# A pool of its own for late latents, one store per latent tile, tables split in the last pair, and the second modulation a step later

## Chip, cores and metric

The kernel runs on one core of one Trainium2 chip. The metric is device microseconds (us) for one execution of the whole kernel: one layer of a bidirectional encoder over two sequences, in one launch.

## What is computed

Two sequences of 1024 tokens with 1024 features go through one layer each, with the same weights and a conditioning vector of their own. Cut to what matters here:

```python
def layer(x, c, ...):
    mod = silu(c) @ w_ada + b_ada                       # six vectors of 1024
    sh1, sc1, ga1, sh2, sc2, ga2 = split(mod, 6)
    h = rmsnorm(x, g_mix) * (1 + sc1) + sh1
    z = h @ w_in
    q_lat, kv_lat, k_pe, f_in = split(z, (256, 128, 64, 512))
    y_mla = mla_group(q_lat, kv_lat, k_pe, ...)         # latent attention, 4 heads
    y_four = fourier_group(f_in, w_four)                # real part of a 2-D FFT per group of 64 features
    x = x + ga1 * (concat(y_mla, y_four) @ w_out)
    h2 = rmsnorm(x, g_ffn) * (1 + sc2) + sh2
    return x + ga2 * ((silu(h2 @ w_gate) * (h2 @ w_up)) @ w_down)
# y = rmsnorm(layer(x, c), g_final) for both sequences
```

## The kernel before

Products are made in three passes. Each fp32 operand is split into a rounded high part and a rest (`split`, L62 to L64: a copy on ScalarE at L63, a subtraction at L64 on VectorE unless another engine is named), and `mm3` (L79 to L81) issues high x high, high x rest and rest x high on TensorE.

**Stage 1**, up to about 216 us, computes h and z. It walks over eight pairs k = 0 to 7 (sequence s = k // 4, index j = k % 4); a pair holds two tiles of 128 tokens that the Fourier transform mirrors on each other. `zboth` makes the latent part of z for both tiles of a pair (448 columns: query latents, key-value latents, rotary key), from sums and differences of the two tiles (`eo`, in the trace `eoh` and `eol`); L467 and L469 bring the result to SBUF, L489 to L495 apply rotation and norm. `latents` transposes the result on TensorE (L519) and splits it (in the trace `lh` and `ll`, in the last pair `lhl`). The two halves, and those of the key-value latents (`kv`), go to DRAM (`lat_d`, `ckv_d`) by one transfer each; they are collected in a list and issued by `flush` (L510). `fourier_in(k, i)` multiplies the even (i = 0) or odd (i = 1) part of a pair with the folded weights and cosines of the feature transform (24 matmuls), and adds the result from PSUM into `zc` (i = 0) or `zs` (i = 1) by two VectorE operations (L545, L546). A product for the row of token 0 and its like (`zoc`, 24 matmuls, L559 to L565) follows the pair where the second sequence begins.

The last pair is written out by hand (from L783): `zboth(7)`, the splits of `zx` and of the cosine half `zh` with the subtraction on GpSimd, the transform of pair 6, the cast of `tcor`, the split of the first table `tb`, the transposes of pair 7, and the transform of pair 7 with the split of `zn`. The raw tables are loaded (L740, L744) into a pool `praw` that is opened at L730, after pool `p1b` has been closed at L728. `p1b` held, among others, the last latents of pairs 2 to 6 (`lat4`, tag `hf`).

**Stage 2** makes the transform over the tokens. `dft(s)` (L931) forms A (cosine part; q = 0, 2, 1 for sequence 0, where 2 is a narrow tile of 48 rows) and B (sine part) with tables `tb[0]` and `tb[1]`. For each q it fills two PSUM banks, `pe` and then `po`, taken in turn from a pool of eight. `zsplit` (L921) splits `zs` (in the trace `zsin`), the subtraction on GpSimd for sequence 0. `fourier_out(s, ..., j, g)` (L1007) multiplies A and B with folded output weights `wm`, in eight steps t per sequence; L1019 to L1022 bring the results to SBUF as `ea` and `ed`, and they go to DRAM (`fo_d`). Between these steps runs the second modulation: `mod2(c)` (L1046) for c = 0 to 7 takes a 1 MB chunk of `w_ada` (tile `wada2`, `wada` in the trace) and issues four matmuls of 32 x 512 (L1054). `mod2(c)` is called behind step t = c + 1 of sequence 0, `mod2(7)` in the middle of `dft(1)`; then L1110 copies the sum to `modrow`, and `mod_vecs` transposes it (L145) and makes the vectors of the second modulation. The chunks 0 to 2 are loaded ahead of `dft(0)` (L1059), behind `wq_l` (L1033).

Attention, output projection and FFN follow; the change doesn't touch them beyond the addresses of the latents in DRAM.

**Order of the work.** Each engine works through its instructions in one order. It follows the order of the code as far as data and buffers allow, and `issue_after` and `behind` hold a part back behind a named instruction. So a tile pool, which decides whose buffer is reused, and the place of a call both move instructions. SyncE (SP) issues nearly all transfers, in order as well: one that waits for its source holds up all behind it.

Of the kernel before, what the change touches and what calls it, by code (L numbers as in the profile page):

```python
# [21 lines left out]
P = 128  # L22
# [31 lines left out]
def hybrid_encoder_kernel(ctx: ExitStack, tc: tile.TileContext, a: dict):  # L54
# [68 lines left out]
    lat_d = [[dram.tile([P, 4, N], F32, name=f"lat_d{s}{i}") for i in range(2)] for s in range(2)]  # L123
    ckv_d = [[dram.tile([P, 8, KVL], F32, name=f"ckv_d{s}{i}") for i in range(2)] for s in range(2)]
# [35 lines left out]

    with ExitStack() as st:
# [34 lines left out]
        mods = {}  # L196
# [25 lines left out]
        def fold_loads():  # L222
            wukT = w.tile([P, HEADS, KVL], F32, tag="lh", name="wukT", bufs=2)
# [225 lines left out]
        def zboth(k, between):  # L449
# [12 lines left out]
            else:  # L462
                if k == 2:
                    st1["lat"] = w2.tile([P, 4, 512], F32, tag="hf", name="lat4", bufs=1)
# [3 lines left out]
            for u in range(2):  # L468
                nc.vector.scalar_tensor_tensor(out=sk[u][:, :DZ], in0=pz[1][:, :DZ], scalar=(0.5, -0.5)[u], in1=sk[1][:, :DZ],  # L469
                                               op0=ALU.mult, op1=ALU.add)  # L470
# [13 lines left out]
        def z_out(k, u, pz, sk, rz):  # L484
# [17 lines left out]
            for i in range(2):  # L502
                st1.setdefault("st", []).append((ckv_d[s][i][:, ti, :], rd(kv[:, i, :])))
# [8 lines left out]
        def latents(k, u):  # L512
# [7 lines left out]
            if k + 1 < nk:  # L520
                lh = w.tile([P, 512], F32R, tag="lh", name="lh", bufs=2)
                ll = w.tile([P, 512], F32R, tag="ll", name="ll", bufs=2)
            else:
                if u == 0:
                    st1["lhl"] = w.tile([P, 4, 512], F32R, tag="hh0", name="lhl")
                lh, ll = (st1["lhl"][:, 2 * u + i, :] for i in range(2))
            split(lh, ll, pl)
            for i, t in enumerate((lh, ll)):
                st1.setdefault("st", []).append((lat_d[s][i][:, :, ti * P : ti * P + P], rd(t).rearrange("p (a b) -> p a b", a=4)))
# [3 lines left out]
        def fourier_in(k, i):  # L533
# [10 lines left out]
            else:  # L544
                nc.vector.tensor_tensor(out=z[:, j, :], in0=z[:, j - 1, :], in1=pc[:, : n1 - n0], op=(ALU.subtract, ALU.add)[i])  # L545
                here["z"] = nc.vector.tensor_tensor(out=z[:, j - 1, :], in0=z[:, j - 1, :], in1=pc[:, : n1 - n0],  # L546
                                                    op=(ALU.add, ALU.subtract)[i]).ins
            if j == 1:
# [10 lines left out]
            if i == 1 and j == 0 and s == 1:  # L559
                po = bank()  # L560
                for c in range(NC):
                    mm3(po[:ZOW, :NZC], zoc[0][:, c, :], zoc[1][:, c, :], wcs_h[:, c, :NZC], wcs_l[:, c, :NZC],
                        c == 0, c == NC - 1)
                nc.vector.tensor_copy(zo, po[:ZOW, :NZC])
                nc.vector.tensor_copy(zc[0][0:1, 1, :], po[0:1, :NZC])  # L565

        def wide(tag, shape=(P, 4, 512)):
            return (w2 if tag == "hf" else w).tile(list(shape), F32, tag=tag, name="wide")
# [9 lines left out]
        wpe = w.tile([P, 2, HEADS * ROPE], F32, tag="lh", name="wpe", bufs=2)  # L578
# [20 lines left out]
        fold_out(1, wo2[0], wuvT, [w.tile([P, 512], F32, tag="ll", name="so", bufs=2) for g in range(2)])  # L599
# [19 lines left out]
        wf.clear()  # L619
        wt = [mod_load(6, cols0, wide("hh0")), mod_load(7, cols0, wada_tile())]  # L620
# [60 lines left out]
        def pair(k):  # L681
# [30 lines left out]
            if k + 1 < nk:  # L712
                next(st1["steps"], None)
# [15 lines left out]
        P2 = ExitStack()  # L729
# [5 lines left out]

        raws = {}
        for k, n in enumerate((NT, 512)):
            for c in range(2):
                raws[k, c] = raw_tile("raw")
                nc.sync.dma_start(raws[k, c][:, :n], a["tcos" if k == 0 else "tsin"][:, c, :])  # L740
        tb[0] = [wr.tile([P, 2, NT], F32R, name=f"tb0{i}") for i in range(2)]
        tcor = wr.tile([P, NTE], F32R, name="tcor")
# [1220 lines left out]
```

## Time and profile before

| | |
|---|---|
| median of 3 runs | 2057.08 us (2056.97 to 2059.08) |
| the profiled execution | 2061.09 us |
| its span in the trace | 2059.3 us |
| granted TensorE clock, mean | 0.995 |
| busy: PE / DVE / ACT / POOL | 2006.8 / 1397.6 / 890.2 / 831.9 us |
| first matmul of `dft(0)` | 215.67 us |
| first matmul of `fourier_out` | 230.69 us |
| first matmuls of the second modulation | 238.41 us |

Engines are named PE (TensorE matmul), DVE (VectorE), ACT (ScalarE), POOL (GpSimd), SP (SyncE). A row of the timeline gives the start in us, the time of the instructions, engine, line, operation, output<-input, shape, and, in square brackets, the idle time ahead and what ended it; x2 means that two like instructions stand in one row. A row of waits gives who waited for whom, the sum in us, the count and the longest. A row of windows gives the stretch, its length, then for PE, PEld (weight load), DVE, ACT and POOL the busy us and the count, the granted PE clock, the share of DMA and GB/s.

### The profile page before, as it was taken

Reading aid. Unit: us, or ns where it says so; the run is one execution under the profiler, and the core shown is the slowest. Engines: PE = TensorE matmul, PEld = TensorE weight load, DVE = VectorE, ACT = ScalarE, POOL = GpSimd, SP = SyncE. Lnnn points to the kernel's source line nnn. Section 1 sums busy time; section 2 is a strip of 40 time slices with the busy share of each in tenths; the row PEclk is TensorE's granted clock in tenths of the full one; section 3 lists DMA queues with packets and bytes.
Section 4 is the critical chain, followed back from the end, with each engine's and each line's share of the span. In section 5 each row is a group of like instructions: output and inputs, shape, how many; then the busy total and the mean of one; then the engine's idle time right before and its main releaser. Section 6 shows DMA issues by size and latency. Waiting matters only on the chain.

```text
span 2059.3 us, 28434 instructions
## 1 busy us (share of the span) xinstructions
PE 2006.8 (97%) x9910; PEld 1641.9 (80%) x9910; DVE 1397.6 (68%) x2071; ACT 890.2 (43%) x1732; POOL 831.9 (40%) x977
## 2 busy tenths in 40 slices
PE   6899899999999999999999999999999999999998
PEld 3778678888888877888888888877788888888876
DVE  4567658666676778667677676678665665667675
ACT  2664435555565564232333365453332333336441
POOL 0564313111313237878779410334544444420142
PEclk9999999999999999999999999999999999999999
DMA  9685884444544375555545587674322322258662
GB/s 387 252 317 178 288 319 112 133 93 104 147 113 143 134 261 200 183 173 179 200 158 185 172 299 254 214 234 166 133 89 90 116 90 103 99 182 277 219 221 96
DMA packets 183548, 376.64 MB, mean 183 GB/s; under 512 B 18508, under 2 KB 58060, under 8 KB 179564
## 3 DMA queue, kind: packets, MB, share of 16 engines
q1 hardware_dynamic: 166060, 321.34, 45.9%
q0 software_dynamic: 17344, 53.49, 8.6%
q8 instruction: 78, 1.28, 0.2%
q14 instruction: 66, 0.54, 0.1%
HBM read 262.75 MB, written 120.39 MB: 186 GB/s over the span
## 4 chain that ended last, share of the span: by engine, by line
PE 55%; DVE 3%; DMA 2%; POOL 1%; issue 1%; SPq 0%; ACT 0%; DVEq 0%; ACTq 0%; POOLq 0%
PE bank L81 19%; PE bank L80 19%; PE bank L79 18%; DVE wl L64 1%; DMA draw<-s_d 1%; DMA draw<-t_d 1%; DVE val L137 1%; DMA val<-x_d 0%; POOL val L137 0%; DVE val L1760 0%; DMA X<-hc_d 0%; ACT wh L63 0%; DVE val L134 0%; POOL rs_y L105 0%; SPq L1719 0%
## 5 line engine op out<-in xcount | busy, mean ns | idle before, releaser
L81 PE MATMUL bank<-H,wl 128*128 128x512 f32 x1232 | 490.4, 398 | 0.2 <-DVE wl L64 0.2
L80 PE MATMUL bank<-H,wh 128*128 128x512 f32 x1232 | 486.2, 395 | 0.3 <-DVE H L64 0.3
L79 PE MATMUL bank<-H,wh 128*128 128x512 f32 x1232 | 483.9, 393 | 2.2 <-DVE val L137 0.9
L79 PEld LDWEIGHTS bank<-H,wh 128*128 128x128 f32 x1232 | 231.3, 188 | 59.9 <-DVE val L137 1.8
L80 PEld LDWEIGHTS bank<-H,wh 128*128 128x128 f32 x1232 | 231.3, 188 | 59.7 <-DVE H L64 0.6
L81 PEld LDWEIGHTS bank<-H,wl 128*128 128x128 f32 x1232 | 231.2, 188 | 53.9 <-DVE wl L64 0.5
L64 DVE TENSOR_TENSOR wl<-draw,wh 128x512 fp32r<-128x512 f32 x286 | 202.1, 742 | 87.5 <-ACT wh L63 87.0
L137 DVE TENSOR_TENSOR val<-bank,val 128x512 f32<-128x512 f32 x200 | 136.6, 689 | 156.8 <-PE bank L81 153.1
L63 ACT CAST wh<-draw 128x512 fp32r<-128x512 f32 x286 | 168.4, 619 | 161.3 <-PE bank L80 90.5
L137 POOL TENSOR_TENSOR val<-val 128x512 f32<-128x512 f32 x58 | 83.3, 1444 | 367.2 <-DVE val L1734 192.9
L80 PE MATMUL bank<-wl,wh 128*128 128x512 f32 x572 | 223.8, 391 | 3.8 <-DVE wl L64 3.8
L79 PE MATMUL bank<-wh 128*128 128x512 f32 x572 | 222.7, 389 | 0.5 <-ACT wh L63 0.5
L63 ACT CAST wh<-rgu 128x512 fp32r<-128x512 f32 x172 | 106.7, 621 | 269.5 <-PE bank L80 209.4
L81 PE MATMUL bank<-wh,wl 128*128 128x512 f32 x572 | 222.7, 389 | 0.0
L63 ACT CAST wh<-val 128x512 fp32r<-128x512 f32 x133 | 82.1, 620 | 269.7 <-PE bank L80 256.2
L64 DVE TENSOR_TENSOR wl<-val,wh 128x512 fp32r<-128x512 f32 x133 | 135.5, 1021 | 75.8 <-ACT wh L63 75.7
L64 DVE TENSOR_TENSOR wl<-rgu,wh 128x512 fp32r<-128x512 f32 x172 | 165.4, 962 | 3.8 <-ACT wh L63 3.8
L134 POOL TENSOR_TENSOR val<-rgu 128x512 f32<-128x512 f32 x80 | 117.8, 1473 | 101.2 <-DMA rgu<-in_wgu_dram 87.0
L80 PEld LDWEIGHTS bank<-wl,wh 128*128 128x128 f32 x572 | 107.3, 188 | 29.4 <-DVE wl L64 7.4
L79 PEld LDWEIGHTS bank<-wh 128*128 128x128 f32 x572 | 107.4, 188 | 23.4 <-ACT wh L63 0.9
L81 PEld LDWEIGHTS bank<-wh,wl 128*128 128x128 f32 x572 | 107.4, 188 | 22.1
L1203 DVE TENSOR_REDUCE mx<-ps_s 128x1 f32<-128x1024 f32 x64 | 78.1, 1221 | 63.4 <-PE ps_s L1198 63.2
(388 smaller groups left out, 4051.5 us busy)
## 6 DMA issues: line engine op xcount, KB each, us to landing
rgu<-in_wgu_dram SPq DMA_DIRECT2D x86, 512.0 KB
draw<-s_d SPq DMA_DIRECT2D x143, 256.0 KB
s_d<-val POOLq DMA_DIRECT2D x88, 256.0 KB, 3.9
draw<-t_d SPq DMA_DIRECT2D x88, 256.0 KB
s_d<-val SPq DMA_DIRECT2D x66, 256.0 KB
draw<-in_w_down_dram SPq DMA_DIRECT2D x55, 256.0 KB
wada<-in_w_ada_dram SPq DMA_DIRECT2D x11, 1024.0 KB
xt<-in_x_dram SPq DMA_DIRECT2D x16, 512.0 KB
```

What stands on the lines that cost most here:

```text
L63: here["a"] = nc.scalar.copy(hi, src).ins
L64: here["v"] = (eng or nc.vector).tensor_tensor(out=lo, in0=src, in1=rd(hi), op=ALU.subtract).ins
L79: nc.tensor.matmul(out, lh, rh, start=first, stop=False, skip_group_check=cont)
L80: nc.tensor.matmul(out, lh, rl, start=False, stop=False, skip_group_check=cont)
L81: here["t"] = nc.tensor.matmul(out, ll, rh, start=False, stop=last, skip_group_check=cont).ins
L134: return eng.tensor_tensor(out=out, in0=x, in1=y, op=ALU.subtract).ins
L137: eng.tensor_tensor(out=out, in0=x, in1=y, op=ALU.add)
L1203: nc.vector.tensor_reduce(out=mx, in_=ps, axis=AX.X, op=ALU.max)
```

## The change

It does these things:

- A pool `p1c` is opened ahead of `p1b` and outlives it to the end of stage 2. It holds what had tag `hf`: the flipped tiles, `lat4`, one wide weight tile, and in stage 2 `wm00`, the first half of the output weights. `p1b` thus ends before the last pair, and `praw` opens with eight raw tiles first.
- Both halves of a latent tile lie in one tile (`lhl`, tag `lq`) and go to DRAM by one transfer; likewise for `kv`. That takes 32 transfers from stage 1.
- Ahead of `zboth(7)` now stand: the loads of the tables, of `wm00` and of `wnr`; the splits of `zx`, `zh` and of the first table; the cast of `tcor`. The subtractions of `zx`, `zh` and `zsin` go from POOL to DVE.
- The transposes of pair 7 go between `fourier_in(7, 0)` and `fourier_in(7, 1)`. The `zoc` product goes from pair 4 to pair 5.
- In stage 2 two of the eight PSUM banks get a tag of their own, `d`, for q = 0 of `dft` and for the sum of the second modulation.
- `mod2(c)` is called behind step t = c + 2, `mod2(6)` and `mod2(7)` in the middle of `dft(1)`. `wq_l` is loaded behind the first three chunks of `w_ada`. The first step of sequence 1 is held behind the copy to `modrow`, and `mod_vecs` behind that step's last product.

```diff
+    w3 = P2.enter_context(tc.tile_pool(name="p1c", bufs=1, side="right", reuse_waits="tile"))
...
-                st1["hf", k] = w2.tile([P, NC, 2, P], F32, tag="hf", name="hf", bufs=1)
+                st1["hf", k] = w3.tile([P, NC, 2, P], F32, tag="hf", name="hf", bufs=1)
...
-            for i in range(2):
-                st1.setdefault("st", []).append((ckv_d[s][i][:, ti, :], rd(kv[:, i, :])))
+            st1.setdefault("st", []).append((ckv_d[s][:, :, ti, :], rd(kv)))
...
-                lh = w.tile([P, 512], F32R, tag="lh", name="lh", bufs=2)
-                ll = w.tile([P, 512], F32R, tag="ll", name="ll", bufs=2)
+                both = w.tile([P, 2, 512], F32R, tag="lq", name="lhl", bufs=2)
...
-            for i, t in enumerate((lh, ll)):
-                st1.setdefault("st", []).append((lat_d[s][i][:, :, ti * P : ti * P + P], rd(t).rearrange("p (a b) -> p a b", a=4)))
+            st1.setdefault("st", []).append((lat_d[s][:, :, :, ti * P : ti * P + P],
+                                             rd(both).rearrange("p i (a b) -> p i a b", a=4)))
...
-            if i == 1 and j == 0 and s == 1:
+            if i == 0 and j == 1 and s == 1:
                 po = bank()
...
+        wmr0 = wm_loads(0, 0, 0)
+        table_load(1)
+        wnr0 = wn_load(0, 0, raw_tile("wnr")[:, :512])
+        split(zxs[0], zxs[1], zx)
+        z0 = zcos_split(0)
+        for c in range(2):
+            split(tb[0][0][:, c, :], tb[0][1][:, c, :], raws[0, c])
+        nc.scalar.copy(tcor, cor[:, :NTE])
         z = zboth(nk - 1, lambda c: flush() if c == 1 else None)
         next(z)
         flush()
-        with behind():
-            split(zxs[0], zxs[1], zx, nc.gpsimd)
-            z0 = zcos_split(0, nc.gpsimd)
-        wm0 = wm_half(0, 0, 0, wr)
-        wm1 = wm_loads(0, 0, 1), wn_load(0, 0, raw_tile("wnr")[:, :512])
+        wm1 = wm_loads(0, 0, 1), wnr0
         next(z, None)
         fourier_in(nk - 2, 0)
-        with behind():
-            nc.scalar.copy(tcor, cor[:, :NTE])
-            for c in range(2):
-                split(tb[0][0][:, c, :], tb[0][1][:, c, :], raws[0, c])
         fourier_in(nk - 2, 1)
+        fourier_in(nk - 1, 0)
         late_latents(nk - 1)
-        fourier_in(nk - 1, 0)
...
+        def bank2(tag="b"):
+            return pp.tile([P, 512], F32, tag=tag, name="bank", bufs=2 if tag == "d" else 6)
...
-                    split(zsin[0][:, c : c + 2], zsin[1][:, c : c + 2], zs[s][:, c : c + 2, :], nc.gpsimd if s == 0 else None)
+                    split(zsin[0][:, c : c + 2], zsin[1][:, c : c + 2], zs[s][:, c : c + 2, :])
...
-                pe, po = bank2(), bank2()
+                pe, po = (bank2("d" if q == 0 else "b") for _ in range(2))
...
-        nc.sync.dma_start(rd(wq_l), wq_d)
...
+        with behind():
+            wm0 = wm_half(0, 0, 0, None, wmr0)
...
         for c in range(3):
             mod2_load(c)
+        nc.sync.dma_start(rd(wq_l), wq_d)
         abn = dft(0)
...
-                    if t > 0:
-                        mod2(t - 1)
+                    if t > 1:
+                        mod2(t - 2)
...
                 def last_mod():
+                    mod2(NC - 2)
                     mod2(NC - 1)
-                    nc.vector.tensor_copy(mr, chunks.pop("ps"))
+                    here["mr"] = nc.vector.tensor_copy(mr, chunks.pop("ps")).ins
```

Two places show what moves. The first is DVE at the end of stage 1, around the last transform of pair 7 (`zc` and `zs` by two additions each) and the first splits of stage 2; rows before, from the split of the first table (`tb_2186`) to that of the second (`tb_2510`):

```order
L64 TENSOR_TENSOR tb_2186<-raw,tb_2185 128x514 x2
L64 TENSOR_TENSOR lhl<-bank,lhl 128x512
L64 TENSOR_TENSOR ll<-bank,lh 128x512
L545 TENSOR_TENSOR zc_111<-zc_111,bank 128x280
L64 TENSOR_TENSOR zn_2193<-zc_110,zn_2192 128x4x24
L546 TENSOR_TENSOR zc_111<-zc_111,bank 128x280
L545 TENSOR_TENSOR zs_113<-zs_113,bank 128x256
L64 TENSOR_TENSOR zn_2193<-zc_111,zn_2192 128x4x24
L546 TENSOR_TENSOR zs_113<-zs_113,bank 128x256
L64 TENSOR_TENSOR wm_2305<-wraw,wm_2304 128x512 x2
L64 TENSOR_TENSOR tb_2510<-raw,tb_2509 128x512 x2
```

The same additions now, up to the split of `wm00`:

```order
L547 TENSOR_TENSOR zc_107<-zc_107,bank 128x280
L548 TENSOR_TENSOR zc_107<-zc_107,bank 128x280
L64 TENSOR_TENSOR lhl<-bank,lhl 128x512 x2
L64 TENSOR_TENSOR zn_2151<-zc_106,zn_2150 128x4x24
L64 TENSOR_TENSOR zn_2151<-zc_107,zn_2150 128x4x24
L547 TENSOR_TENSOR zs_109<-zs_109,bank 128x256
L548 TENSOR_TENSOR zs_109<-zs_109,bank 128x256
L64 TENSOR_TENSOR zsin_2459<-zs_108,zsin_2458 128x512 x2
L64 TENSOR_TENSOR tb_2465<-raw,tb_2464 128x512 x2
L64 TENSOR_TENSOR wm_2470<-wraw,wm_2470 128x512 x2
```

The split of the first table has left this place: its two subtractions now stand some 14 rows ahead of `zc`, beside the rows in which the result of `zboth(7)` leaves PSUM. `zsin` is new on DVE, and `wm00` went behind the second table.

The second place is PE where the second modulation begins, among the products of `fourier_out` (`wm` with A, then with B); rows before, from the last three products of its second step to the first of the third:

```order
L79 MATMUL bank<-wm_2606,B_2529 128x512
L80 MATMUL bank<-wm_2607,B_2529 128x512
L81 MATMUL bank<-wm_2606,B_2530 128x512
L1054 MATMUL bank<-wada_2521,scT_2515 32x512 x4
L79 MATMUL bank<-wm_2304,A_2527 128x512
```

Now the first of them stands here, behind the first six products of the first step:

```order
L79 MATMUL bank<-wm_2470,A_2488 128x512
L80 MATMUL bank<-wm_2470,A_2488 128x512
L81 MATMUL bank<-wm_2470,A_2489 128x512
L1070 MATMUL bank<-wada_2481,scT_2475 32x512
L79 MATMUL bank<-wm_2567,B_2490 128x512
```

One of the four matmuls of `mod2(0)` has come 20 products forward, into the first step; the other three went back behind the third step. Before, all four stood together behind the second.

More of the change, by code (lines that the diff above doesn't have):

```diff
@@ L547, in fourier_in @@
                                                     op=(ALU.add, ALU.subtract)[i]).ins
+            if i == 0 and j == 1 and s == 1:
+                po = bank()
+                for c in range(NC):
+                    mm3(po[:ZOW, :NZC], zoc[0][:, c, :], zoc[1][:, c, :], wcs_h[:, c, :NZC], wcs_l[:, c, :NZC],
+                        c == 0, c == NC - 1)
+                nc.vector.tensor_copy(zo, po[:ZOW, :NZC])
+                nc.vector.tensor_copy(zc[0][0:1, 1, :], po[0:1, :NZC])
             if j == 1:
@@ L558, in fourier_in @@
                     nc.vector.tensor_copy(zoc[k][:, :, 2 * s : 2 * s + 2], rd(eo[1][k][:, :, 0:2]))
-            if i == 1 and j == 0 and s == 1:
[L560 to L565, printed above, removed]
         def wide(tag, shape=(P, 4, 512)):
-            return (w2 if tag == "hf" else w).tile(list(shape), F32, tag=tag, name="wide")
+            return (w3 if tag == "hf" else w).tile(list(shape), F32, tag=tag, name="wide")
         cols0 = [(0, 2048)]
@@ L751, in zcos_split @@
             return z
-        zn = [wr.tile([P, 4, NY2], F32R, name=f"zn{i}") for i in range(2)]
         def nyq_split():
@@ L895, in stage3_loads @@
         S["ld"] = last
-        S["ld2"] = [(rd(lat[i]), lat_d[0][i][:, 2:4, :]) for i in range(2)] + [(rd(ckv[i]), ckv_d[0][i]) for i in range(2)]
+        S["ld2"] = [(rd(lat[i]), lat_d[0][:, i, 2:4, :]) for i in range(2)] + [(rd(ckv[i]), ckv_d[0][:, i]) for i in range(2)]
         return rc, rs
@@ L1003, in prep_wm @@
                             st.enter_context(tc.issue_after(ins))
[L1004 to L1005 removed]
+                    halves = [wm_half(s, g, h, w, raw[h]) for h in range(2)]
+                    wms[s][g] = halves, list(wn)[-1]
         def fourier_out(s, ABn, j, g):
```

78 lines of the change are left out of this document (46 added, 32 removed).

## Prediction

> **What bounds the kernel now.** I read the page first: the busy times (part 1) and the chain that ended last (part 4).
>
> ```profile
> PE 2006.8 (97%) x9910; PEld 1641.9 (80%) x9910; DVE 1397.6 (68%) x2071; ACT 890.2 (43%) x1732; POOL 831.9 (40%) x977
> PE 55%; DVE 3%; DMA 2%; POOL 1%; issue 1%; SPq 0%; ACT 0%; DVEq 0%; ACTq 0%; POOLq 0%
> ```
>
> PE is busy for 2006.8 of 2059.3 us, so all its gaps together are 52.5 us, and PE leads the chain by far. The number and shapes of the matmuls stay as they are. So the time can only change by PE's gaps, by its clock, and by how closely small matmuls stand together. The instructions move from stage 1 to the start of sequence 1 in stage 2, about 60 to 310 us. Next I asked for PE's waits in that window (sum, count, longest):
>
> ```profile
> PE bank L519 <- DVE lat L494: 3.4, 2, 1.8
> PE bank L79 <- DVE zs L546: 2.5, 1, 2.5
> PE bank L80 <- DVE tb L64: 2.0, 2, 1.1
> PE bank L384 <- POOL rs_r L109: 1.5, 1, 1.5
> PE bank L1054 <- DMA wada<-in_w_ada_dram: 1.3, 1, 1.3
> PE bank L145 <- DVE modrow L1110: 1.0, 1, 1.0
> ```
>
> Those on `zs`, `tb`, `wada` and `modrow`, 6.8 us together, lie where the change works. The others (`lat`, `rs_r`) belong to pairs 1 to 3, whose instructions only move by a few places. Third, PE's timeline around those waits:
>
> ```profile
> 215.67 0.28 PE L79 MATMUL bank<-tb,zh 128*128 128x258 f32 x1
> 217.24 0.39 PE L80 MATMUL bank<-tb,zh 128*128 128x258 f32 x1 [0.94 <-DVE tb L64]
> 220.24 0.58 PE L79 MATMUL bank<-tb,zh 128*128 128x256 f32 x1 [2.50 <-DVE zs L546]
> 228.33 0.39 PE L80 MATMUL bank<-tb,zsin 128*128 128x256 f32 x1 [1.06 <-DVE tb L64]
> 238.41 1.06 PE L1054 MATMUL bank<-wada,scT 128*32 128x512 f32 x8 [1.27 <-DMA wada<-in_w_ada_dram]
> 277.38 1.06 PE L1054 MATMUL bank<-wada,scT 128*32 128x512 f32 x8
> 279.49 0.66 PE L145 MATMUL bank<-ident,modrow 128*128 128x128 f32 x4 [1.04 <-DVE modrow L1110]
> ```
>
> The transform begins at 215.67, stops for 0.94 us, and after two matmuls more for 2.50 us. The cause is in DVE's and POOL's rows there:
>
> ```profile
> 213.80 3.39 DVE L64 TENSOR_TENSOR tb<-raw,tb 128x514 fp32r<-128x514 f32 x2 [1.92 <-ACT tb L63]
> 217.11 0.68 DVE L64 TENSOR_TENSOR lhl<-bank,lhl 128x512 fp32r<-128x512 f32 x1
> ...
> 219.19 0.41 DVE L545 TENSOR_TENSOR zs<-zs,bank 128x256 f32<-128x256 f32 x1
> 219.60 0.26 DVE L64 TENSOR_TENSOR zn<-zc,zn 128x96 fp32r<-128x96 f32 x1
> 219.78 0.41 DVE L546 TENSOR_TENSOR zs<-zs,bank 128x256 f32<-128x256 f32 x1
> 213.65 2.99 POOL L64 TENSOR_TENSOR zh<-zc,zh 128x512 fp32r<-128x512 f32 x2
> ```
>
> DVE splits the first table until 217.19 and comes to `zs` at 219.19 only, although the product for `zs` left PE by about 215.8. The second bank of the transform (`po`) is the one that `zs` still has to leave, so PE stands until 220.19. Fourth, the windows there (granted PE clock third from the end):
>
> ```profile
> 220.20:223.60 3.40, 3.36 (x15) 3.24 (x16) 0.25 (x1) 0.70 (x2) 0.00 (x0) 0.50 0.99 284
> 223.60:227.20 3.60, 3.46 (x28) 3.12 (x26) 2.60 (x4) 3.60 (x9) 2.45 (x2) 1.00 1.07 330
> ```
>
> After the double stop PE works 3.40 us at half clock: 15 matmuls in 3.40 us, 0.227 us each, against 28 in 3.46 busy us at full clock, 0.124 each. That loss is in no row of waits.
>
> **The change, part by part.**
>
> *The table's split goes into pair 7.* It leaves the place ahead of `zs`, and POOL's `zx` and `zh` splits go to DVE ahead of it. What is late next is `zs` itself. From the end of its product at 215.8, two additions of 0.41 us end near 216.7; the six products of `pe` (0.12 us each from 215.67) end near 216.4. I leave a stop of 0.4. So 0.94 + 2.50 - 0.4 = **3.0 us gained**. The bounds: 3.4, if the additions are hidden, and 0.9, if only the first stop goes.
>
> *The half clock.* In this window stops of up to 1.84 us (the 1.8 of the `lat` row) left the clock at full; with 0.4 left I expect none. 15 x (0.227 - 0.124) = **1.5 us gained**; bounds 0 and 1.5. [...]
>
> *The second table and `zsin`.*
>
> ```profile
> 225.74 2.54 DVE L64 TENSOR_TENSOR tb<-raw,tb 128x512 fp32r<-128x512 f32 x2 [0.87 <-ACT tb L63]
> 224.75 2.98 POOL L64 TENSOR_TENSOR zsin<-zs,zsin 128x512 fp32r<-128x512 f32 x2 [5.00 <-ACT zsin L63]
> 223.35 1.51 DVE L64 TENSOR_TENSOR wm<-wraw,wm 128x512 fp32r<-128x512 f32 x2 [3.16 <-ACT wm L63]
> ```
>
> With POOL at work beside it, a subtraction of 512 columns took DVE 1.27 us (2.54 / 2); without it, 0.76 (1.51 / 2). Now DVE does `zsin` and `tb`, four at 0.76, right behind `zs`: 216.7 + 3.0 = 219.7. PE comes to B after 42 products of A (5.0 us from 215.7) and the stop, at about 221.1. So the **1.06 us** go, with 1.4 us to spare; at 1.27 us each they would end at 221.8 and 0.7 would be left. The cover for `wm00`, which is now third (until 221.3), is longer: PE wants it at about 224, behind B. The added work in pairs 6 and 7 (`zx` and `zh`, 1.9 us; the table, 1.5) lies ahead of what `zboth(7)` needs:
>
> ```profile
> 190.96 1.28 DVE L64 TENSOR_TENSOR eol<-xT,eoh 128x512 fp32r<-128x512 f32 x2
> 197.16 0.36 PE L79 MATMUL bank<-wz_h,eoh 128*128 128x448 f32 x1
> ```
>
> `eol` was ready at 192.2, wanted at about 197.2. Behind 1.9 us more, and behind two copies from PSUM and a split that now stand ahead of it (some 2 us), it comes near 196. I take 0; each us beyond that margin costs one.
>
> *The chunks of `w_ada`.*
>
> ```profile
> 223.52 2.99 SPq L510 DMA_DIRECT2D lat_d<-lhl  x4
> 229.19 0.33 SPq L1033 DMA_DIRECT2D wq_l<-wq_d  x1
> 230.99 1.38 SPq L1059 DMA_DIRECT2D wada<-in_w_ada_dram  x3
> ```
>
> Before, the last stores of latents held `wq_l`, and it and three small loads came ahead of the chunks: issued at 230.99, the first was there at 238.4, 7.4 us later. Now the transposes of pair 7 end at about 212.9, their splits near 214.8; two stores, three small loads at about 0.45 us, and the chunks are issued near 216.7. By the same 7.4 us the first lands at about 224.1; the stores in front (1 MB) stand in for `wq_l` (0.75 MB). The first matmul of `mod2(0)` has moved forward as well: A and B are 66 products of 0.12 us, six of `wm` 0.23 us each, so PE comes to it near 225.4. So the **1.27 us** go, with some 1.3 us to spare. If the stores slow the chunk by 3 us, up to 2 come back.
>
> *A group of four cut in two.*
>
> ```profile
> 9.81 1.06 PE L214 MATMUL bank<-wada,scT 128*32 128x512 f32 x6 [1.43 <-DMA wada<-in_w_ada_dram]
> 11.22 1.05 PE L214 MATMUL bank<-wada,scT 128*32 128x512 f32 x2
> ```
>
> These are the same shape in stage 1: one matmul (x2) takes as long as three (x6) or four (x8). Cutting off one of the four of `mod2(0)` **costs 1.0 us**; bounds 0.3 and 1.1.
>
> *The end of the modulation.* The copy to `modrow` (0.68 us on DVE) no longer stands behind an addition of `ed`; the transposes still follow directly. The stop goes from 1.04 to about 0.75: **0.3 gained**, between 0 and 1.
>
> *Free edits.* The 32 stores fewer, the move of `zoc` (24 products from pair 4 to 5) and `wq_l` behind the chunks (wanted only at step 4) touch no wait of the list; ±0.5. For the waits of pairs 1 to 3 (3.4 and 1.5) I take no change, with 2 us either way as bound, since only whole stops of 1.5 to 1.8 us could come or go there.
>
> **Sum.** 3.0 + 1.5 + 1.06 + 1.27 - 1.0 + 0.3 = 6.1 us. The profiled execution took 2061.09 us and would take 2055.0. It lies 4.0 us above the median of the runs, so I subtract the same from the median: 2057.08 - 6.1 = **2051.0 us**, 0.30% faster. About 0.2%, 4.1 us, is what a measurement of this kernel can tell from no change.
>
> **The rivals.**
>
> *The chunk comes late for a product that now stands early.* The window between the issue of the chunks and the first one's use:
>
> ```profile
> 230.90:238.40 7.50, 6.24 (x26) 4.35 (x24) 7.50 (x14) 5.68 (x10) 0.22 (x1) 1.00 0.94 344
> ```
>
> The matmul of `mod2(0)` was the 27th product of `fourier_out`; now it is the seventh, and everything on PE waits behind it. For it speaks that DMA was 94% busy there at 344 GB/s, so 1 MB of stores more ahead costs about 3 us. At 3 to 4 us late the sum falls to 2 to 3: 2053 to 2055.
>
> *The stops only change place.* The table's split then makes pair 7 wait, or `zs` still comes behind other work on DVE (`lhl` and `zn` stand between `zc` and `zs`). If 2.5 us of stop and the half clock stay, 3.6 of the 4.5 us are lost: about 2054.6. If the tables land as late as before, which would mean that the new pool doesn't free their space sooner, only 1.06 + 1.27 - 1.0 + 0.3 = 1.6 us stay: 2055.5, or up to 2057 if the second table is late too. Against it speaks that the loads now stand behind the key-value latents of pair 5, about 10 us earlier than 205.6, and that the additions for `zs` are the only ones that wait for PE's last product.
>
> *Slower.* One mechanism: SP is in order, so the chunks leave behind the last stores. If those still leave as late as before, the chunks are issued at 230.99 in the time of the trace, or 225 with the transform shortened, and land at 232.4 to 238.4. PE then stands from 225.4 for 7 to 13 us in place of 1.27. Added to 2051.0 these are 2058 to 2064; it is slower than before from a landing at about 231.5. The splits of pair 7, not behind the table any more, speak against it.
>
> **How the numbers follow.** The forecast holds with a chance of 0.58: 2051.0, from 2048 (2 us from pairs 1 to 3 and some of the bounds) to 2052.9. The late chunk has 0.17 (2053 to 2055), the stops that change place 0.15 (2054.6 to 2057), the slower one 0.10, of which 0.08 lie above 2061.2. So the range goes from 2047.5 to 2056.5; it leaves out the slower rival, some of the stops and little below. Faster by over 0.2% (under 2053.0): 0.58. Within 0.2%: 0.17 + 0.15 + 0.02 = 0.34. Slower: 0.08.
>
> **What would show it.** In the profile of the changed kernel: no wait on `tb` in either transform, one on `zs` of about 0.4 us at the sixth product, and a granted clock of 1.00 in the 3.4 us behind it; no wait on `wada` at the first matmul of the second modulation, but two groups of about 1 us for `mod2(0)`; about 0.75 us ahead of the transposes of `modrow`; the waits on `lat` and `rs_r` as they were. A wait over 1 us on `wada`, on `zs`, or on `eol` near 197 us would prove a step wrong.

## The result, and the profile after

The changed kernel took 2052.22 us (median of 13 runs, 2048.45 to 2056.76), the kernel before 2057.26 us (13 runs, 2056.08 to 2063.6). The ratio is 0.997 with a 95% interval from 0.9961 to 0.9978: 4.5 to 8.0 us faster. Forecast were 2051.0 us and 6.1 us less.

The busy times hardly differ. Those of the changed kernel, from the first part of its page:

```profile
PE 2006.0 (98%) x9910; PEld 1641.6 (80%) x9910; DVE 1397.2 (68%) x2076; ACT 890.5 (43%) x1732; POOL 827.0 (40%) x972
```

PE's work is the same to 1 us (2006.8 before), in 9910 matmuls both times; what changed lies in its gaps and its clock. PE's waits in the window from 60 to 310 us:

```profile
PE bank L522 <- DVE lat L498: 3.4, 2, 1.8
PE bank L1070 <- DMA wada<-in_w_ada_dram: 1.6, 1, 1.6
PE bank L388 <- POOL rs_r L109: 1.4, 1, 1.4
PE bank L145 <- DVE modrow L1132: 0.8, 1, 0.8
...
PE bank L79 <- DVE zs L548: 0.2, 1, 0.2
```

The 2.5 us on `zs` have become 0.2, the 2.0 on `tb` are gone, `lat` and `rs_r` are as they were. But 1.6 stand on `wada`, where 1.3 stood. PE's timeline at those places:

```profile
215.92 0.28 PE L79 MATMUL bank<-tb,zh 128*128 128x258 f32 x1
217.05 0.39 PE L79 MATMUL bank<-tb,zh 128*128 128x256 f32 x1 [0.25 <-DVE zs L548]
224.34 0.40 PE L79 MATMUL bank<-wm,A 128*128 128x512 f32 x1
227.49 1.04 PE L1070 MATMUL bank<-wada,scT 128*32 128x512 f32 x2 [1.59 <-DMA wada<-in_w_ada_dram]
236.34 1.06 PE L1070 MATMUL bank<-wada,scT 128*32 128x512 f32 x6
274.15 0.66 PE L145 MATMUL bank<-ident,modrow 128*128 128x128 f32 x4 [0.82 <-DVE modrow L1132]
301.82 0.39 PE L1216 MATMUL ps_s<-lat,qa 128*128 128x512 f32 x1
```

The last row is the first product of attention, the first one behind stage 2. In the kernel before, the first product of stage 1's feature transform and this one stood here:

```profile
61.34 0.29 PE L79 MATMUL bank<-wcs_h,eoh 128*128 128x280 f32 x1
308.00 0.50 PE L1194 MATMUL ps_s<-lat,qa 128*128 128x512 f32 x1 [0.67 <-ACT ed L1028]
```

Five such rows cut the trace into four stretches. From kernel to kernel, where nothing was changed in them, their lengths repeat within 0.1 us in (b) and (d), and within 0.8 in (a), apart from a half clock in pair 2 that two traces have and that adds 1.5 to 2. (c) holds the wait for the first chunk of `w_ada`, which moves with what comes before it; with this wait taken off, (c) repeats within 0.1 us where its order is the same. Whole runs of one kernel spread over 8 us; so the experiments are read by the stretches, each from one trace.

| stretch | before | after | difference |
|---|---|---|---|
| (a) first `wcs` product to first product of `dft(0)` | 154.33 | 154.42 | +0.09 |
| (b) to the first product of `fourier_out` | 15.02 | 8.42 | -6.60 |
| (c) to the transposes of `modrow` | 48.80 | 49.81 | +1.01 |
| (d) to the first product of attention | 28.51 | 27.67 | -0.84 |
| sum | 246.66 | 240.32 | -6.34 |

So 6.3 us were won, nearly all in the transform, and 1.0 was given back behind it.

### The profile page after: what moved, and what is told of

The parts are those of the page before. It is cut to its first block, busy times and chain, and to the rows that moved or that the text cites. A ratio compares the mean times of both kernels' runs of the same rounds, so it can differ in the third digit from the quotient of the medians.

```text
span 2049.5 us, 28369 instructions
## 1 busy us (share of the span) xinstructions
PE 2006.0 (98%) x9910; PEld 1641.6 (80%) x9910; DVE 1397.2 (68%) x2076; ACT 890.5 (43%) x1732; POOL 827.0 (40%) x972
## 4 chain that ended last, share of the span: by engine, by line
PE 55%; DVE 3%; DMA 2%; issue 1%; POOL 1%; ACT 0%; SPq 0%; DVEq 0%; ACTq 0%; POOLq 0%
PE bank L81 18%; PE bank L79 18%; PE bank L80 18%; DVE wl L64 1%; DVE val L137 1%; DMA draw<-s_d 1%; POOL val L137 0%; DMA val<-x_d 0%; DVE val L1782 0%; DMA draw<-t_d 0%; ACT wh L63 0%; DVE val L134 0%; POOL rs_y L105 0%; DVE H L64 0%; DMA rgu<-in_wgu_dram 0%
## 5 line engine op out<-in xcount | busy, mean ns | idle before, releaser
L64 DVE TENSOR_TENSOR wl<-val,wh 128x512 fp32r<-128x512 f32 x133 | 130.8, 985 | 77.3 <-ACT wh L63 77.3
```

The costliest lines, as they stand in the source:

```text
L64: here["v"] = (eng or nc.vector).tensor_tensor(out=lo, in0=src, in1=rd(hi), op=ALU.subtract).ins
```

## The experiments

Each kernel is the changed one with the edit shown. Ratios are to the kernel before, run on the same chip; the chips differ from group to group.

| kernel | (a) | (b) | (c) | (d) | sum | ratio (95%) |
|---|---|---|---|---|---|---|
| changed | 154.42 | 8.42 | 49.81 | 27.67 | 240.32 | 0.997 (0.9961 to 0.9978) |
| e4_late | 153.92 | 8.72 | 50.49 | 27.67 | 240.80 | 0.9978 (0.9967 to 0.9989) |
| e3_pool | 154.06 | 8.43 | 52.14 | 27.67 | 242.30 | 0.9977 (0.9968 to 0.9986) |
| e13_loads | 156.16 | 8.41 | 48.14 | 27.68 | 240.39 | 0.995 (0.9934 to 0.9966) |
| e11_old_pool | 154.25 | 10.14 | 49.33 | 27.67 | 241.39 | 0.9954 (0.9936 to 0.9972), two runs only |
| e12_old_dve | 154.17 | 10.45 | 48.66 | 27.67 | 240.95 | 0.9972 (0.9959 to 0.9984) |
| e14_all | 155.53 | 10.08 | 50.44 | 27.69 | 243.74 | 0.9992 (0.9977 to 1.0008) |
| e15_order | 159.34 | 8.37 | 50.48 | 27.68 | 245.87 | 0.9989 (0.9978 to 1.0001) |
| e5_dve4 | 154.16 | 10.84 | 48.39 | 27.67 | 241.06 | 0.9979 (0.997 to 0.9988) |
| e1_hold | 154.06 | 8.41 | 49.00 | 27.67 | 239.14 | 0.9969 (0.9957 to 0.9981) |
| e10_best | 153.60 | 8.42 | 48.72 | 27.68 | 238.42 | 0.9949 (0.9936 to 0.9963) |
| e2_wq | 156.00 | 8.41 | 54.21 | 27.69 | 246.31 | 0.9986 (0.9976 to 0.9996) |
| e7_two | 153.97 | 8.34 | 53.37 | 27.69 | 243.37 | 0.9992 (0.9981 to 1.0003) |

The ratios don't rank these kernels as the sums do: e11_old_pool has a lower ratio than the changed kernel and a sum that is 1.1 us longer, e13_loads a lower ratio at the same sum. Their intervals overlap the changed kernel's. So differences of 1 or 2 us between the experiments are readings of single traces, which the measured times don't confirm.

### Which part of the table work made the stops

**e4_late**

```diff
-        for c in range(2):
-            split(tb[0][0][:, c, :], tb[0][1][:, c, :], raws[0, c])
-        nc.scalar.copy(tcor, cor[:, :NTE])
...
         fourier_in(nk - 2, 0)
+        with behind():
+            nc.scalar.copy(tcor, cor[:, :NTE])
+            for c in range(2):
+                split(tb[0][0][:, c, :], tb[0][1][:, c, :], raws[0, c])
```

> Only the split of the first table (and the cast of tcor) goes back behind the transform of pair 6, as before; its subtractions still run without POOL beside them. Theory: it is the length of the split (3.39 us beside POOL's subtractions, 1.4 without) as much as its place that made the stops; then zs is ready about 1.4 us later, PE stops about 1.5 us on zs, the clock stays full, and the time is 1 to 1.5 us above the changed kernel (about 2053.4 us). Rival: the place alone decides; both stops and the half clock come back, 4 to 5 us above the changed kernel (about 2057).

(b) grew by 0.3 us. Both were wrong: the late split took 1.30 us for two at 211.15, and DVE had time for it ahead of `zs`.

**e3_pool**

```diff
-        split(zxs[0], zxs[1], zx)
-        z0 = zcos_split(0)
+        split(zxs[0], zxs[1], zx, nc.gpsimd)
+        z0 = zcos_split(0, nc.gpsimd)
...
-                    split(zsin[0][:, c : c + 2], zsin[1][:, c : c + 2], zs[s][:, c : c + 2, :])
+                    split(zsin[0][:, c : c + 2], zsin[1][:, c : c + 2], zs[s][:, c : c + 2, :], nc.gpsimd if s == 0 else None)
```

> Only the subtractions of zx, zh and zsin go back from DVE to POOL; their places in the code stay. Theory: with the table split early these subtractions lie off the path, so the time is that of the changed kernel within 0.5 us (about 2052.2), even though the second table's two subtractions take 2.5 us beside POOL instead of 1.4. Rival: DVE slowed by POOL makes the second table or zs late again, with a stop of 1 us or more and 2053.5 or above.

(b) is the same to 0.01 us, as the theory had it. (c) is 2.3 us longer, not foreseen: in the second transform PE waited for a split of A, and then went on at half clock. The wait stands in e14_all and e15_order as well (1.82 us each, at full clock), the other two kernels of the table with `zsin` on POOL, and is 0.57 us at most in the rest; how `zsin` brings it about wasn't traced. PE's row and the window there:

```profile
267.58 0.38 PE L79 MATMUL bank<-tb,zh 128*128 128x256 f32 x1 [1.81 <-DVE A L64]
```

```profile
267.40:270.60 3.20, 3.02 (x11) 2.76 (x12) 1.76 (x5) 0.86 (x2) 0.00 (x0) 0.56 1.05 384
```

**e13_loads**

```diff
-        table_load(0)
-        cor = raw_tile("raw")
-        nc.sync.dma_start(cor[:, :NTE], a["tcor"])
...
+        z = zboth(nk - 1, lambda c: flush() if c == 1 else None)
+        next(z)
+        flush()
+        table_load(0)
+        cor = raw_tile("raw")
+        nc.sync.dma_start(cor[:, :NTE], a["tcor"])
         wmr0 = wm_loads(0, 0, 0)
         table_load(1)
...
-        z = zboth(nk - 1, lambda c: flush() if c == 1 else None)
-        next(z)
-        flush()
```

With the tables, the loads for `wm00` and `wnr` and the calls of the splits come behind the first part of `zboth(7)` too.

> The changed kernel with only the loads of the tables put back, behind the stores of pair 5, with the splits wherever their data lets them stand (all subtractions on DVE). e11_old_pool and e12_old_dve put only the splits back and brought back 1.7 and 2.0 us of the 6.6 us that the transform had gained. Theory: the early loads alone are worth little as long as the split stands early in DVE's and ScalarE's order; the stretch from the first product of the transform to the first of fourier_out is under 9.3 us. Rival: late loads hold ScalarE's and DVE's queues, the additions for zs come late, and the stretch is over 10.5 us.

The theory held: (b) is 8.41. The 1.7 us in (a) come at 82 to 87 us, from a half clock in pair 2 (products of 448 columns 0.37 us apart, 0.20 in the changed kernel), over 100 us ahead of the edit (see the last section). And (c) is 48.14, the shortest of all: PE doesn't wait for the first chunk. The rows that differ are those of pair 6's latents; first the changed kernel's, then e13_loads's:

```profile
202.35 1.04 PE L522 MATMUL bank<-ident,lat 128*128 128x128 f32 x8
211.84 1.45 DVE L64 TENSOR_TENSOR lhl<-bank,lhl 128x512 fp32r<-128x512 f32 x2 [0.19 <-ACT lhl L63]
```

```profile
205.71 0.69 DVE L64 TENSOR_TENSOR lhl<-bank,lhl 128x512 fp32r<-128x512 f32 x1
206.56 2.36 SPq L513 DMA_DIRECT2D lat_d<-lhl  x2
221.40 1.32 SPq L1075 DMA_DIRECT2D wada<-in_w_ada_dram  x3
```

In the changed kernel pair 6's latents are transposed by 203.4, but split only behind the norm of pair 7, at 211.84, and stored from 212.56. In e13_loads they are transposed by 204.8 and split at 205.71 and 207.69; the stores leave from 206.56, and the chunks 4.06 us behind the first product of the transform instead of 6.53. In e11_old_pool and e12_old_dve below, where the loads stay early and the splits of `zx`, `zh` and the table go back, pair 6's split is late as well (210.83 and 213.90); in e14_all and e15_order, where both go back, its stores leave from 205.28 and 205.02. So it is the early loads that hold up pair 6's stores, and with them the chunks; by which way wasn't traced. Without its half clock, e13_loads's sum is about 1.7 us below the changed kernel's: as long as the splits stand early, the early loads show no gain.

**e11_old_pool**

```diff
-        split(zxs[0], zxs[1], zx)
-        z0 = zcos_split(0)
-        for c in range(2):
-            split(tb[0][0][:, c, :], tb[0][1][:, c, :], raws[0, c])
-        nc.scalar.copy(tcor, cor[:, :NTE])
...
         next(z)
         flush()
+        with behind():
+            split(zxs[0], zxs[1], zx, nc.gpsimd)
+            z0 = zcos_split(0, nc.gpsimd)
...
         fourier_in(nk - 2, 0)
+        with behind():
+            nc.scalar.copy(tcor, cor[:, :NTE])
+            for c in range(2):
+                split(tb[0][0][:, c, :], tb[0][1][:, c, :], raws[0, c])
```

> The changed kernel with the splits of zx, zh and the first table back in their old places in the last pair, and the subtractions of zx and zh on POOL again; PE's order is the changed kernel's. e3_pool and e4_late showed that neither the subtractions on POOL nor the late table alone bring the stops back. Theory: it takes both, with POOL's zx and zh beside the table's split on DVE; then that split takes 2.5 to 3.4 us again, PE stops 1.5 us or more on zs or tb, and the stretch from the first product of the transform to the first of fourier_out is over 10 us (kernel before 15.0, changed 8.4). Rival: the stops came from the transposes of pair 7 standing ahead of its transform (their lhl splits behind the table on DVE), which this kernel doesn't undo; then the stretch stays under 9.3 us.

**e12_old_dve** differs from it in two lines:

```diff
-            split(zxs[0], zxs[1], zx, nc.gpsimd)
-            z0 = zcos_split(0, nc.gpsimd)
+            split(zxs[0], zxs[1], zx)
+            z0 = zcos_split(0)
```

> As e11_old_pool, but with the subtractions of zx and zh on DVE. If POOL beside DVE is what makes the table's split long, it takes 1.3 to 1.5 us here, but DVE has 1.9 us more to do ahead of zs; the stretch is then 9 to 10.5 us, and shorter than e11_old_pool's. If the place alone decides, it is as long as e11_old_pool's or longer.

The stretches are 10.14 and 10.45: 1.7 and 2.0 us came back. The theory's 10 us were just reached, but for another reason than it gave. e12 is no shorter than e11, which was the sign that the place decides here and not POOL. DVE's and POOL's rows of e11_old_pool:

```profile
209.62 1.30 DVE L64 TENSOR_TENSOR tb<-raw,tb 128x514 fp32r<-128x514 f32 x2 [0.83 <-ACT tb L63]
```

```profile
213.35 2.53 POOL L64 TENSOR_TENSOR zh<-zc,zh 128x512 fp32r<-128x512 f32 x2
```

The table's split takes 1.30 us and comes before POOL's work; what is late is `lhl`, `zn` and `zs` behind it, and PE stops 1.1 us on `zs` and 0.6 on `zh`. In e12_old_dve it stops 2.3 us on `zs`, behind DVE's own `zx` and `zh`.

**e14_all** joins e13's edit of the loads, e11's of the splits, and e3's of `zsin`:

```diff
         next(z)
         flush()
+        table_load(0)
...
+        table_load(1)
+        with behind():
+            split(zxs[0], zxs[1], zx, nc.gpsimd)
+            z0 = zcos_split(0, nc.gpsimd)
```

> The changed kernel with everything on the tables undone together: loads behind the stores of pair 5, splits of zx, zh and the first table in their old places (ScalarE casts zx and zh ahead of the table again), subtractions of zx, zh and zsin on POOL. Theory: the stops of the kernel before need all of this together, above all the table's split on DVE beside POOL's zx and zh; then the split takes 2.5 us or more again, PE stops 2 us or more before the second bank, and the stretch from the first product of the transform to the first of fourier_out is 12 us or more (before 15.0, changed 8.4); half clock may or may not follow the stops. Rival: part of the gain comes from the order of pair 7's transposes and transform, which stays as changed here; then the stretch stays under 11 us.

**e15_order** is e14_all with one line moved:

```diff
-        fourier_in(nk - 1, 0)
         late_latents(nk - 1)
+        fourier_in(nk - 1, 0)
```

> e14_all with the transposes of pair 7 ahead of its transform again, the last part of the change around the tables. e14_all left one stop of 1.91 us on zs and a stretch of 10.1 us from the first product of the transform to the first of fourier_out. Theory: in the kernel before, the two lhl splits of pair 7 on DVE (0.7 us each) and the table's split came ahead of zc and zs in one row; with the transposes back the additions of zc move behind the lhl splits and the stretch is as long or up to 1.5 us longer (10 to 11.6), and what is missing to 15.0 is the half clock (1.4) and POOL's zx and zh falling on the table's split, which in e14_all fell on the norm instead. Rival: this order alone is the rest, and the stretch is 13 us or more.

e14's stretch (b) is 10.08, as its rival had it, and (a) grew by 1.1. e15's (b) is 8.37, outside theory and rival: the stop moved ahead of the transform. PE's and DVE's rows of e15_order:

```profile
213.00 1.02 PE L522 MATMUL bank<-ident,lat 128*128 128x128 f32 x4 [1.40 <-DVE lat L498]
```

```profile
208.45 1.45 DVE L498 TENSOR_SCALAR lat<-lat,rs_r 128x256 f32<-128x256 f32 x1 [3.26 <-POOL rs_r L109]
```

The transposes of pair 7 wait for the norm of its latents on DVE (1.45 us, while POOL does `zx` and `zh`; 0.68 and 0.34 in the changed kernel), three stops of 2.8 us together, and half clock follows from 214 to 217 us (products of 280 columns 0.23 us apart, 0.13 behind it). So (a) and (b) have to be added: 169.35 before, 162.84 changed; e4, e3 162.6 and 162.5; e13 162.9 without its half clock in pair 2; e11 and e12 164.4 and 164.6; e14 165.6; e15 167.7. In these two stretches no part that was undone alone is worth 0.5 us. With the splits in their old place 1.6 to 1.8 us come back, with loads and `zsin` as well 2.8, with the order of pair 7 too 4.9 of 6.5. The parts cover for each other. The steps of 1 to 2 us are above the 0.8 by which (a) repeats, but each stands on one or two traces, and the 1.6 us that are left weren't traced further.

### The chunks of the second modulation

**e2_wq**

```diff
         zsplit(0, z0)
+        nc.sync.dma_start(rd(wq_l), wq_d)
...
         for c in range(3):
             mod2_load(c)
-        nc.sync.dma_start(rd(wq_l), wq_d)
```

> The changed kernel with the load of wq_l (768 KB) ahead of the three chunks, as before, held by the last stores of latents. Theory: the chunks are issued some 3 us later, behind the landing of the stores, and the first lands 3 to 5 us later than in the changed kernel (227.4); the matmul of mod2(0), which stands a few products later here, then waits 2 to 5 us, and the stretch from the first product of fourier_out to the transposes of modrow grows by 1 us or more above the changed kernel's 49.8. Rival: the order of the loads is hidden, and the stretch stays within 0.5 us.

**e7_two**

```diff
-            st1.setdefault("st", []).append((ckv_d[s][:, :, ti, :], rd(kv)))
+            for i in range(2):
+                st1.setdefault("st", []).append((ckv_d[s][:, i, ti, :], rd(kv[:, i, :])))
...
-            st1.setdefault("st", []).append((lat_d[s][:, :, :, ti * P : ti * P + P],
-                                             rd(both).rearrange("p i (a b) -> p i a b", a=4)))
+            for i in range(2):
+                st1.setdefault("st", []).append((lat_d[s][:, i, :, ti * P : ti * P + P],
+                                                 rd(both[:, i]).rearrange("p (a b) -> p a b", a=4)))
```

> The changed kernel with two transfers for each latent tile and for each kv tile again (the shared tile stays), 32 transfers more in stage 1. Theory: SP then issues twice as many stores ahead of the chunks, each waiting for the one eight places ahead; the chunks leave 0.5 to 2 us later (changed kernel: 6.5 us behind the first product of the transform) and the stretch from the first product of fourier_out to modrow's transposes grows by as much. Rival: it is the bytes of the stores (2 MB at about 290 GB/s) and not their number that hold the chunks, and the chunks leave within 0.3 us of the changed kernel's time.

SP's rows of the changed kernel, of e2_wq and of e7_two (start of the issues, time of them):

```profile
212.56 1.27 SPq L513 DMA_DIRECT2D lat_d<-lhl  x2
217.32 1.36 SPq L513 DMA_DIRECT2D lat_d<-lhl  x2
218.77 1.77 SPq L1056 DMA_DIRECT2D scT<-sc_d  x1
220.59 1.23 SPq L1058 DMA_DIRECT2D bT<-in_bT_dram  x1
222.45 1.34 SPq L1075 DMA_DIRECT2D wada<-in_w_ada_dram  x3
```

```profile
228.10 1.32 SPq L1076 DMA_DIRECT2D wada<-in_w_ada_dram  x3
```

```profile
218.89 2.87 SPq L514 DMA_DIRECT2D lat_d<-lhl  x4
224.11 2.14 SPq L1077 DMA_DIRECT2D wada<-in_w_ada_dram  x3
```

In the kernel before, SP's waits behind the chunks are of this kind: the first three `wraw` wait 0.6, 0.2 and 0.7 us for `wq_l`, `scT` and `bT`, and the first `fo_d` 1.9 us for the first chunk, each of them eight transfers ahead.

Counted from the first product of the transform, the chunks leave at 6.53 us (changed), 9.29 (e2_wq) and 10.41 (e7_two); before, at 15.3. PE then waits 1.59, 3.73 and 3.58 us, the last two with half clock behind them (the single matmul takes 1.91 and 1.92 us there, 1.04 in the changed kernel), so that (c) is 4.4 and 3.6 us longer. Both theories hold in kind. e2's size is as expected; e7's is twice its upper bound: the number of stores counts, not only their bytes. The place of `wq_l` is worth 4.4 us and the single store 3.6 in these traces, more than half of the gain each, and the ratios of the two kernels, 0.9986 and 0.9992, agree. But the waits alone grew by 2.1 and 2.0 us; the rest is mostly the half clock behind them, seen in one trace each.

### The early matmul of `mod2(0)`

**e1_hold**

```diff
+            with tc.issue_after(here["t"]) if c == 0 else ExitStack():
                 for j in range(4):
                     nc.tensor.matmul(chunks["ps"][32 * j : 32 * j + 32, :], scT[:, c, :], wt[:, j, :], ...)
```

> Only the changed kernel's matmuls of mod2(0) are held behind the last product of the third step, so that all four stand together again. Theory: the single early matmul costs its wait for the chunk (1.59 us) and a group of its own (1.0), so this kernel is 2.6 us faster than the changed one (about 2049.6 us) and PE waits for no chunk. Rival: the DVE work for the first step (second half of the weights, ready at 227.9, and wn, at 228.5) is late as well, and PE waits for it once the chunk is out of the way; then only 1.0 to 1.4 us are won (about 2051).

**e10_best** has this and

```diff
-                pe, po = (bank2("d" if q == 0 else "b") for _ in range(2))
+                pe, po = (bank2("d" if q == 0 and s == 0 else "b") for _ in range(2))
```

> As e1_hold (the four matmuls of mod2(0) together, behind the third step), and in the second transform the bank po of q = 0 comes from the six banks, not from the two of tag d, one of which the sum of the modulation holds. In e1_hold the first edit won 2.0 us between the first step and the second chunk, and 1.2 of it were lost again in the second transform, where PE waited 0.57 us for a split of A. Theory: that wait comes from the bank, so here the stretch from the first product of fourier_out to the transposes of modrow is about 48.0 us or less (changed kernel 49.8, e1_hold 49.0), and the time is 1.5 to 2 us below the changed kernel's. Rival: the order that the second transform then takes costs as much in another place, and the stretch stays near 49.

e1_hold won 0.8 us in (c), less than both said. PE's stops there:

```profile
223.78 0.50 PE L79 MATMUL bank<-wm,B 128*128 128x512 f32 x1 [0.48 <-ACT wm L789]
```

```profile
262.56 0.35 PE L79 MATMUL bank<-tb,zh 128*128 128x256 f32 x1 [0.57 <-DVE A L64]
```

The first is the rival's: the next operand is late by 0.48. The second comes from the second transform, which the edit reordered. In e10_best the bank takes that stop away, but 0.37 us on `wn` and 0.24 on a later chunk come up, and (c) is 48.72: 1.1 us shorter than in the changed kernel, where 1.8 or more were expected. Over the four stretches e10_best is 1.9 us below the changed kernel (0.8 of it in (a), whose order is the same, so chance). Its ratio of 0.9949 is the lowest of all, with e13_loads's 0.995 beside it; its interval just touches the changed kernel's.

### One stop, and the clock

**e5_dve4**

```diff
-                nc.vector.tensor_tensor(out=z[:, j, :], in0=z[:, j - 1, :], in1=pc[:, : n1 - n0], ...)
+                with tc.issue_after(late) if late is not None else ExitStack():
+                    nc.vector.tensor_tensor(out=z[:, j, :], in0=z[:, j - 1, :], in1=pc[:, : n1 - n0], ...)
...
         with behind():
             nyq_split()
+        with behind():
+            for _ in range(4):
+                here["v"] = nc.vector.tensor_tensor(out=zxs[1], in0=zx, in1=rd(zxs[0]), op=ALU.subtract).ins
...
-        fourier_in(nk - 1, 1)
+        fourier_in(nk - 1, 1, here["v"])
```

> The changed kernel with four extra DVE subtractions (zx's low half, written four times with the same values, 0.65 us each) ahead of zs, so that PE stops once, for about 2.4 us, on zs, with no stop on a table ahead of it. If one stop of 2.4 us halves the clock by itself, the granted clock is 0.50 for some 3.4 us behind it and the time is 2.2 + 1.4 = 3.6 us above the changed kernel (about 2055.8). If the clock needs a longer idle stretch, as the two stops of the kernel before made together (3.4 us), it stays at 1.00 and the time is 2.2 us above (about 2054.4).

PE's row and the window behind it:

```profile
220.98 0.39 PE L79 MATMUL bank<-tb,zh 128*128 128x256 f32 x1 [2.67 <-DVE zs L549]
```

```profile
221.00:224.40 3.40, 3.40 (x28) 3.40 (x29) 3.40 (x5) 1.16 (x4) 2.67 (x2) 1.00 0.97 283
```

One stop of 2.67 us left the clock at 1.00, and (b) grew by 2.4 us, just by the stop. The median time, 2055.81 us, is what the other alternative gave. But the kernel before took 2059.69 us on this chip, 2.4 more than beside the changed kernel, so the two medians can't be set side by side; the trace decides, for its one execution.

## Why the prediction was right

- **The table's split and `zs`**: 3.0 us forecast; 0.94 + 2.50 became 0.25, 3.2. Right, and the stop of 0.25 stands where it was expected, behind the sixth product. But the prediction put it on the table's place and on POOL's sharing; undone alone, the place (e4_late) and POOL's work (e3_pool) bring back 0.3 us and nothing. Loads, splits, POOL's work and the order of pair 7 cover for each other.
- **Half clock**: 1.5 forecast. The 3.40 us behind the stop are now at 1.00:

```profile
217.40:220.80 3.40, 3.40 (x31) 3.40 (x30) 3.40 (x5) 1.96 (x6) 2.53 (x2) 1.00 1.05 326
```

  31 matmuls stand where 15 stood, and from the seventh product of A to the first of B it takes 4.41 us instead of 5.87: 1.46 won. Right for this trace; it isn't a property of the order alone (last section).
- **Second table**: 1.06 forecast, and no wait is left; its two subtractions took 2.38 us, not 1.5 (POOL was at work on `wnr` beside them), and still ended ahead of B at 221.46. What (b) won beyond these three terms, 6.60 - 3.2 - 1.46 - 1.06 = 0.9 us, belongs to the stops too: before, the product behind each starts 0.15 us later than the idle time says, the next one 0.1 or more, and one of B's first products came 0.3 us late in a gap that the list of waits doesn't have.
- **Chunks of `w_ada`**: the step that failed, by the sign that the prediction itself had named. 1.27 us were to go; the wait became 1.59. The step put the issue near 216.7 with three small loads at 0.45 us each and 1 MB of stores in front. The issue was at 222.45: the prediction had left out that the early loads would hold up pair 6's latents (e13_loads); their stores leave at 212.56 only, so 2 MB of latents stand in front, and `scT`, `bT` and `gT` took 1.77, 1.23 and 0.48. From issue to use it was 5.0 us, not 7.4. The rival "the chunk comes late" came true in part: 1.6 us late, where it had put 3 to 4. This wait is all that (c) missed: without it (c) is 48.22, and the forecast, 48.80 - 1.27 + 1.0 - 0.3, is 48.23. In e4_late, e11_old_pool, e12_old_dve and e13_loads, where the wait is 2.27, 1.11, 0.44 and nothing, the rest of (c) is 48.22, 48.22, 48.22 and 48.14.
- **The group cut in two**: 1.0 forecast; the single matmul took 1.04, and the next product started 0.97 behind it.
- **`modrow`**: 1.04 became 0.82, forecast 0.75.
- **Missed**: stretch (d), 0.84 us. The wait of 0.67 on `ed` ahead of attention is gone, in every kernel of the table; the prediction's list of waits ends one row above it. Which part of the change did it wasn't tested.

The miss on the chunks (1.6) and on (d) (0.8) and the restarts (0.9) nearly cancel, so 6.1 forecast stand against 6.34 in the stretches. That closeness is luck. The mechanism in the transform was right, and one term, the chunks, had the wrong sign: the wait grew instead of going.

## What to carry to other kernels

When a load is moved up behind stores, count what is still to be stored when it is issued, not only what stands next to it in the queue, and ask what your own edit does to those stores: here `wq_l` and the number of stores were worth 4.4 and 3.6 us with the half clock behind them, and the late stores of pair 6 the 1.6 us of PE's wait. A gain that several edits share can show up in none of them alone; undo them one by one and then together, and compare stretches between two fixed products, because a stop can move across the border of one stretch, as 2.8 us did in e15_order. A single small matmul placed early on PE took a group time of its own here, 1.04 us, where three or four together take 1.06, and made the delay of its operand PE's, 1.59 us.

## What the runs showed of the hardware

The length of a stop did not by itself decide whether the clock fell. A stop of 2.67 us (e5_dve4) left it at 1.00, and behind one of 2.3 (e12_old_dve) the products of 256 columns stood 0.12 us apart, as at full clock. 1.81 us on a split of A brought 0.56 (e3_pool); 1.82 us at the same place left 1.00 (e14_all) and products 0.12 us apart (e15_order). Stops of 0.73, 0.70 and 1.40 close together were followed by products of 280 columns 0.23 us apart, against 0.13 from 217.1 us on (e15_order). And the stop of 1.4 to 1.5 us on `rs_r`, which every kernel has, was followed by half clock in e2_wq and e13_loads (products of 448 columns 0.37 us apart for 0.20), and by 1.00 from 86.0 to 89.4 us in the kernel before and the changed one. The stop of 1.82 us in e14_all, and the window from its end:

```profile
270.31 0.35 PE L79 MATMUL bank<-tb,zh 128*128 128x256 f32 x1 [1.82 <-DVE A L64]
```

```profile
270.20:273.60 3.40, 3.29 (x21) 1.98 (x22) 1.75 (x4) 0.86 (x2) 0.00 (x0) 1.00 0.92 331
```

The stop on `rs_r` in e2_wq, and the window behind it:

```profile
84.00 0.43 PE L388 MATMUL bank<-ident,rs_r 128*128 128x128 f32 x2 [1.50 <-POOL rs_r L109]
```

```profile
86.00:89.40 3.40, 3.40 (x14) 3.06 (x11) 1.99 (x4) 1.27 (x3) 0.00 (x0) 0.59 1.04 423
```

Behind 3.58 us (e7_two) and 3.73 (e2_wq) half clock came both times: the single matmul of `mod2(0)` took 1.92 and 1.91 us instead of 1.04, and e2_wq was granted 0.65 from 236.60 to 240.00 us. What decides between stops of like length, no run here shows. For a prediction it means that a half clock seen in one trace, here 1.5 us, is a term with a chance, not a sure one.
